# Queries of two latent heads projected and their rotary parts transposed together

## The chip, the cores and the metric

The kernel runs on one core of one Trainium2 chip. The metric is the device time of one execution in microseconds (us), as a median of several executions; lower is better. The engines are named as the profile names them: PE (TensorE, matmuls), PEld (its weight loads), DVE (VectorE), ACT (ScalarE), POOL (GpSimd) and SP (SyncE, which issues DMAs).

## The reference

One decoder layer over 1024 tokens of 1024 features: a SwiGLU block, a mixer with two groups of heads, and a second SwiGLU block. The change lies in the second group of the mixer, multi-head latent attention with four heads of 128 + 64 query columns:

```python
q = (_rms(cq, q_a_norm) @ w_q_b).reshape(B, S, H, MLA_QK_DIM)          # H = 4, 192 columns a head
kv = (_rms(ckv, kv_a_norm) @ w_kv_b).reshape(B, S, H, MLA_NOPE + MLA_V_DIM)
k = jnp.concatenate([k_nope, k_pe], axis=-1)
q, k = _rms(q, q_g), _rms(k, k_g)
q = jnp.concatenate([q[..., :MLA_NOPE], _rope(q[..., MLA_NOPE:], pos)], axis=-1)
k = jnp.concatenate([k[..., :MLA_NOPE], _rope(k[..., MLA_NOPE:], pos)], axis=-1)
```

followed by causal softmax attention of each head. `cq` has 256 features, so a query tile is a sum over two blocks of 128. Every product of exact operands is made of three matmuls on a high and a low part of each operand.

## The kernel before

The program is one long list that a scheduler puts in order at build time; each engine then runs its own list, and semaphores hold an instruction back until what it reads or overwrites is ready. The stages follow each other: first SwiGLU, projections, twelve attention heads, output projection, second SwiGLU.

The attention stage walks over `order`, a list of (head, item): eight dilated heads with eight pairs of tiles each, then four latent heads with eight query tiles each (the last head in reverse). An item has four steps: scores `s` (lines 838 and 890), exponential `e` (846, 903), transposes `t` (854, 914) and values `v` (864, 929); `t` runs three items behind `s`, and `v` four. Between the steps `behind` advances jobs. A job is a generator with a start, an end and a number of steps, and at each call it is moved on in proportion to the place reached in `order`. `merge` (lines 1258 to 1260) is such a job: it combines the near and far halves of the dilated heads. `prep_mla` is another: it prepares the latent heads, from `MSTART` on, with 75 steps spread up to one head before the end of the list.

For each head and each half of the tokens (four tiles, `th`) `prep_mla` does the following, with a `yield` after each piece. It projects the keys and values (two banks of PSUM, 256 columns a tile, `products`, lines 122 to 126) and takes the squares of the keys on ACT (1157). It runs what is left of the half before (`late`: transposes of the keys). It projects the queries, two tiles of 192 columns to a bank and two banks a half; DVE multiplies a bank with the gain (1172) and ACT squares it (1175). Behind the first query bank DVE scales the keys (1179), ACT copies the values (1183) and POOL scales the keys' rotary part (1185). DVE rotates the queries' rotary part in six instructions (1101 to 1106). PE transposes the queries' first 128 columns (`turn_nope`, line 1052) and then the rotary 64 (`turn_rope`, 1052), each with four transposes; ACT copies the high part of the rotary result to the upper 64 partitions of `qs` (1117), and DVE writes the low part to the other 64 (1118). POOL makes the queries' inverse norms (1192 to 1194) and rotates the keys (1101 to 1106). `late` transposes the keys in the same way and has two DMAs on POOL's queue swap halves of `k1` into `k2` (1205, 1206).

All tiles of 4 KB a partition come from a pool of 47 buffers (`slot`), and PSUM has 8 banks (`ps`).

Of the kernel before, what the change touches and what calls it, by code (L numbers as in the profile page):

```python
# [10 lines left out]
F32 = mybir.dt.float32  # L11
# [41 lines left out]
MSTART = 6.5  # L53
# [8 lines left out]
def tile_layer(ctx: ExitStack, tc: tile.TileContext, x, g1n, mixn, g2n, wg1, wu1, wd1, wg2, wu2, wd2,  # L62
# [985 lines left out]
    def four_turns(src, rows_, hi, lo):  # L1048

        tp = ps()  # L1050
        for i in range(4):
            nc.tensor.transpose(tp[:rows_, i * P:(i + 1) * P], src(i), ident)  # L1052
        if rows_ == P:
            split(hi, lo, tp)
        return tp
# [40 lines left out]
    def rotary(eng, y, th, o):  # L1096

        cos, sin = mla["cs"][:, 4 * th:4 * th + 4, 0:32], mla["cs"][:, 4 * th:4 * th + 4, 32:64]
        a, b = y[:, :, 0:32], y[:, :, 32:64]
        w = tmp([P, 2, 4, 32])  # L1100
        eng.tensor_tensor(o[:, :, 0:32], a, cos, op=ALU.mult)
        eng.tensor_tensor(w[:, 0], b, sin, op=ALU.mult)
        eng.tensor_tensor(o[:, :, 32:64], b, cos, op=ALU.mult)
        eng.tensor_tensor(w[:, 1], a, sin, op=ALU.mult)
        eng.tensor_tensor(o[:, :, 0:32], o[:, :, 0:32], w[:, 0], op=ALU.subtract)
        eng.tensor_tensor(o[:, :, 32:64], o[:, :, 32:64], w[:, 1], op=ALU.add)
# [3 lines left out]
    def turn_nope(y, th, nope):  # L1110
        sl = slice(th * 512, (th + 1) * 512)
        four_turns(lambda i: y[:, i, :NOPE], P, nope[0][:, sl], nope[1][:, sl])

    def turn_rope(ro, th, rope):
        sl = slice(th * 512, (th + 1) * 512)
        tp = four_turns(lambda i: ro[:, i, :], ROPE, None, None)
        nc.scalar.activation(rope[:ROPE, sl], tp[:ROPE, :], AF.Copy)
        nc.vector.tensor_tensor(rope[ROPE:, sl], tp[:ROPE, :], rope[:ROPE, sl].bitcast(F32), op=ALU.subtract)

    def mla_head(h):  # L1120
        qn, kn = ((slot([P, 1024], F32R), slot([P, 1024], F32R)) for _ in range(2))
        qs, k1, k2 = (slot([P, 1024], F32R) for _ in range(3))
        vh = slot([P, NT, P])
        rq = [(small(4), small(4)) for _ in range(2)]
# [16 lines left out]
        return qn, kn, qs, k1, k2, vh, rq  # L1141

    def prep_mla():


        late = iter(())
        for h in range(MH):
            cT, wq, wkv = mla["c"], mla["wq"], mla["wkv"]
            qn, kn, qs, k1, k2, vh, rq = mla_head(h)
            for th in range(2):  # L1150
                yk, yq, ro, ss, pk = slot([P, 4, QK]), slot([P, 4, QK]), tmp([P, 4, ROPE]), small(4), []
# [12 lines left out]
                sq = small(4)  # L1164
                for b in range(2):
                    pq = ps()
                    for i in range(2):
                        t, o = 4 * th + 2 * b + i, pq[:, i * QK:(i + 1) * QK]
                        products(o, [(cut(cT[k], t * P, (t + 1) * P), cut(wq[k], h * QK, (h + 1) * QK))
                                     for k in range(2)])  # L1170
                    yv = yq[:, 2 * b:2 * b + 2, :]
                    nc.vector.tensor_tensor(yv, pq[:, :2 * QK].rearrange("p (i c) -> p i c", i=2),
                                            mla["gq"][:, None, :].to_broadcast([P, 2, QK]), op=ALU.mult)
                    for i in range(2):
                        nc.scalar.activation(pq[:, i * QK:(i + 1) * QK], pq[:, i * QK:(i + 1) * QK], AF.Square,
                                             accum_out=sq[:, 2 * b + i:2 * b + i + 1])
                    if b == 0:
                        for i in range(4):
                            nc.vector.scalar_tensor_tensor(
# [275 lines left out]
```

## Time and profile before

| | us |
|---|---|
| median of 3 runs | 1834.58 (1834.56 to 1834.69) |
| the profiled execution | 1836.06 |
| span of its instructions | 1834.3 |
| PE busy | 1807.4, 9040 instructions |
| DVE busy | 1240.9, 2375 instructions |
| ACT busy | 785.9, 1794 instructions |
| POOL busy | 305.8, 528 instructions |

The profiled execution took 1.5 us more than the median, of which 1.8 us lie around the span. Busy time counts an engine's instructions from start to modelled end, so matmuls that overlap in the pipeline count once, and a PE that is 99% busy can still wait for up to some 0.15 us at a time without a gap in the count. How often matmuls start says more than how long one lasts.

### The profile page before, as it was taken

What the parts mean: (1) busy time and instruction counts of PE and PEld (TensorE: products, weight loads), DVE (VectorE), ACT (ScalarE), POOL (GpSimd) and SP (SyncE); (2) the same over time, 40 slices, a digit from 0 to 9 for tenths busy, and PEclk for the clock granted to TensorE, in tenths of its full rate; (3) what the DMA queues carried; (4) which work ended last, traced back from release to release, by engine and by line L of the source; (5) the groups of instructions that cost most, each with busy time, mean ns of one, the idle gap of its engine ahead of it and who ended that gap; (6) DMA issues with size and microseconds to landing.
All of it is one profiled execution on the core that took longest, in us unless ns stands there. A gap on an engine that the chain in (4) does not pass through costs nothing.

```text
span 1834.3 us, 25184 instructions
## 1 busy us (share of the span) xinstructions
PE 1807.4 (99%) x9040; PEld 1532.6 (84%) x9040; DVE 1240.9 (68%) x2375; ACT 785.9 (43%) x1794; POOL 305.8 (17%) x528
## 2 busy tenths in 40 slices
PE   8999999999999999999999999999999999999999
PEld 6888888888888888889998988888888888888887
DVE  6878776677967364337878783458777666687771
ACT  7532233333454343236876672364232333343540
POOL 3111110000000213332455530211111001000000
PEclk9999999999999999999999999999999999999999
DMA  7435452228943241023311332344345223387412
GB/s 287 163 113 185 145 187 90 98 77 292 342 127 92 99 131 35 29 69 116 87 33 36 84 113 95 125 167 137 132 165 190 86 93 120 134 300 272 127 51 92
DMA packets 95077, 243.82 MB, mean 133 GB/s; under 512 B 12934, under 2 KB 18776, under 8 KB 94952
## 3 DMA queue, kind: packets, MB, share of 16 engines
q1 hardware_dynamic: 72744, 167.12, 27.4%
q0 software_dynamic: 22208, 75.09, 12.0%
q8 instruction: 71, 1.16, 0.3%
q14 instruction: 54, 0.44, 0.1%
HBM read 172.34 MB, written 65.63 MB: 130 GB/s over the span
## 4 chain that ended last, share of the span: by engine, by line
PE 90%; DVE 3%; DMA 2%; ACT 2%; issue 1%; POOL 1%; SPq 0%; POOLq 0%; DVEq 0%; ACTq 0%
PE ps L122 20%; PE ps L124 20%; PE ps L126 20%; PE ps L524 7%; PE ps L523 7%; PE ps L522 7%; PE ps L864 2%; PE ps L929 1%; PE ps L890 1%; PE ps L838 1%; PE ps L854 1%; PE ps L1052 1%; DMA slot<-in_wu_dram 1%; PE ps L178 1%; ACT slot L101 1%
## 5 line engine op out<-in xcount | busy, mean ns | idle before, releaser
L122 PE MATMUL ps<-slot,slot 128*128 128x512 f32 (+3 forms) x1712 | 657.6, 385 | 3.1 <-DVE slot L218 1.6
L124 PE MATMUL ps<-slot,slot 128*128 128x512 f32 (+3 forms) x1712 | 654.0, 382 | 0.0
L126 PE MATMUL ps<-slot,slot 128*128 128x512 f32 (+3 forms) x1712 | 654.0, 382 | 0.0
L122 PEld LDWEIGHTS ps<-slot,slot 128*128 128x128 f32 x1712 | 322.0, 188 | 65.9 <-DVE slot L218 2.1
L126 PEld LDWEIGHTS ps<-slot,slot 128*128 128x128 f32 x1712 | 322.0, 188 | 61.8
L124 PEld LDWEIGHTS ps<-slot,slot 128*128 128x128 f32 x1712 | 322.2, 188 | 60.5
L102 DVE TENSOR_TENSOR slot<-slot,slot 128x512 fp32r<-128x512 f32 (+1 forms) x428 | 293.7, 703 | 40.6 <-ACT slot L101 38.8
L101 ACT ACTIVATE slot<-slot 128x512 fp32r<-128x512 f32 (+1 forms) x428 | 259.6, 638 | 98.9 <-PE ps L524 49.0
L101 ACT ACTIVATE slot<-tmp 128x512 fp32r<-128x512 f32 x258 | 160.8, 625 | 317.0 <-DVE tmp L332 137.3
L523 PE MATMUL ps<-slot,slot 128*128 128x512 f32 x616 | 239.8, 390 | 0.0
L524 PE MATMUL ps<-slot,slot 128*128 128x512 f32 x616 | 239.6, 389 | 0.0
L522 PE MATMUL ps<-slot,slot 128*128 128x512 f32 x616 | 237.2, 389 | 0.0
L102 DVE TENSOR_TENSOR slot<-tmp,slot 128x512 fp32r<-128x512 f32 x258 | 176.4, 686 | 21.7 <-ACT slot L101 21.6
L523 PEld LDWEIGHTS ps<-slot,slot 128*128 128x128 f32 x616 | 115.7, 188 | 24.1
L524 PEld LDWEIGHTS ps<-slot,slot 128*128 128x128 f32 x616 | 115.7, 188 | 23.9
L522 PEld LDWEIGHTS ps<-slot,slot 128*128 128x128 f32 x616 | 115.7, 188 | 23.8
L609 ACT ACTIVATE tmp<-tmp 128x512 f32<-128x512 f32 x76 | 48.1, 632 | 152.7 <-DVE tmp L601 72.8
L530 DVE SCALAR_TENSOR_TENSOR slot<-ps,slot 128x512 f32<-128x512 f32 x56 | 37.4, 687 | 81.1 <-PE ps L524 80.9
L846 ACT ACTIVATE slot<-slot,tmp 128x256 f32<-128x256 f32 (+1 forms) x128 | 59.7, 468 | 27.2 <-DVE tmp L839 26.4
L136 POOL TENSOR_TENSOR small<-small,neghalf 128x1 f32<-128x1 f32 (+2 forms) x68 | 66.8, 984 | 5.0
L592 DVE TENSOR_TENSOR tmp<-tmp,ps 128x512 f32<-128x512 f32 x44 | 30.2, 686 | 51.2 <-ACT tmp L588 50.7
L864 PE MATMUL ps<-slot,slot 128*128 128x64 f32 x432 | 56.3, 269 | 2.2 <-DVE slot L856 1.6
(180 smaller groups left out, 1962.8 us busy)
## 6 DMA issues: line engine op xcount, KB each, us to landing
tmp<-act SPq DMA_DIRECT2D x154, 256.0 KB
slot<-in_wg_dram SPq DMA_DIRECT2D x56, 512.0 KB
slot<-in_wu_dram SPq DMA_DIRECT2D x56, 512.0 KB
act<-slot POOLq DMA_DIRECT2D x54, 512.0 KB, 4.6
slot<-in_wd_dram SPq DMA_DIRECT2D x40, 512.0 KB
act<-slot POOLq DMA_DIRECT2D x34, 256.0 KB, 3.3
slot<-in_x_dram SPq DMA_DIRECT2D x16, 512.0 KB
x_mid<-slot POOLq DMA_DIRECT2D x16, 512.0 KB, 3.5
```

The source lines that it names most:

```text
L101: nc.scalar.activation(hi, src, AF.Copy)
L102: return nc.vector.tensor_tensor(lo, src, hi.bitcast(F32), op=ALU.subtract)
L122: pin(nc.tensor.matmul(pt, ah, bh, start=first and i == 0, stop=False, skip_group_check=not first))
L124: pin(nc.tensor.matmul(pt, ah, bl, start=False, stop=False, skip_group_check=not first))
L126: pin(nc.tensor.matmul(pt, al, bh, start=False, stop=i == total - 1, skip_group_check=not first))
L136: nc.gpsimd.tensor_tensor(r, r, neghalf[:, :w], op=ALU.pow)
L522: nc.tensor.matmul(banks[i], ah, w[:, 0, :], start=first and k == 0, stop=False, skip_group_check=not first)
L523: nc.tensor.matmul(banks[i], ah, w[:, 1, :], start=False, stop=False, skip_group_check=not first)
L524: nc.tensor.matmul(banks[i], al, w[:, 0, :], start=False, stop=k == KD - 1, skip_group_check=not first)
L609: nc.scalar.activation(q, q, AF.Silu)
L846: nc.scalar.activation(self.p[:, e, :w], self.p[:, e, :w], AF.Exp, bias=self.m[e], scale=-1.0, accum_out=self.den[e])
L864: nc.tensor.matmul(po[:, e * HD:(e + 1) * HD], self.pt[:, n * P:(n + 1) * P], self.head["values"](self.far, self.j, e, j - nb + 1), start= ...
```

## The change

Heads are prepared in pairs. For an even head, the tiles of both heads' queries are allocated together (`queries`), and for each half of the tokens the queries of this head and the next are projected in one product of 384 columns a tile (four banks, one a tile, two blocks of 128 features, three matmuls each). The gain, the squares and the rotation work on both heads at once in pieces of the same number of elements as before. The rotary parts of both heads (2 x 64 columns) of a tile are transposed by one transpose; the result has the first head in the lower 64 partitions and the second in the upper, and ACT and DVE then write high and low parts for each head. For an odd head only keys and values are left. `MSTART` goes from 6.5 to 6.

```diff
-MSTART = 6.5
+MSTART = 6
...
-    def turn_rope(ro, th, rope):
+    def turn_rope(src, th, ropes):
+
         sl = slice(th * 512, (th + 1) * 512)
-        tp = four_turns(lambda i: ro[:, i, :], ROPE, None, None)
-        nc.scalar.activation(rope[:ROPE, sl], tp[:ROPE, :], AF.Copy)
-        nc.vector.tensor_tensor(rope[ROPE:, sl], tp[:ROPE, :], rope[:ROPE, sl].bitcast(F32), op=ALU.subtract)
+        tp = four_turns(src, ROPE * len(ropes), None, None)
+        for i, rope in enumerate(ropes):
+            own, other = (slice(j * ROPE, (j + 1) * ROPE) for j in (i, 1 - i))
+            nc.scalar.activation(rope[own, sl], tp[own, :], AF.Copy)
+            nc.vector.tensor_tensor(rope[other, sl], tp[own, :], rope[own, sl].bitcast(F32), op=ALU.subtract)
...
+    def queries():
+        return (slot([P, 1024], F32R), slot([P, 1024], F32R)), slot([P, 1024], F32R), [(small(4), small(4)) for _ in range(2)]
...
-            qn, kn, qs, k1, k2, vh, rq = mla_head(h)
+            if h % 2 == 0:
+                two = [queries() for _ in range(2)]
+            kn, k1, k2, vh = mla_head(h, *two[h % 2])
...
-                for b in range(2):
-                    pq = ps()
-                    for i in range(2):
-                        t, o = 4 * th + 2 * b + i, pq[:, i * QK:(i + 1) * QK]
-                        products(o, [(cut(cT[k], t * P, (t + 1) * P), cut(wq[k], h * QK, (h + 1) * QK))
-                                     for k in range(2)])
...
+                rok = tmp([P, 4, ROPE])
+                if h % 2:
+                    keys()
                     yield
...
+                    rotary(nc.gpsimd, yk[:, :, None, NOPE:], 4 * th, rok[:, :, None])
+                else:
+                    yq, ro, sq = [slot([P, 2, 2, QK]) for _ in range(2)], tmp([P, 4, 2, ROPE]), [small(4) for _ in range(2)]
+                    for i in range(4):
+                        t, pq = 4 * th + i, ps()
+                        products(pq[:, :2 * QK], [(cut(cT[k], t * P, (t + 1) * P), cut(wq[k], h * QK, (h + 2) * QK))
+                                                  for k in range(2)])
+                        nc.vector.tensor_tensor(yq[i // 2][:, i % 2], pq[:, :2 * QK].rearrange("p (j c) -> p j c", j=2),
+                                                mla["gq"][:, None, :].to_broadcast([P, 2, QK]), op=ALU.mult)
+                        for j in range(2):
+                            o = pq[:, j * QK:(j + 1) * QK]
+                            nc.scalar.activation(o, o, AF.Square, accum_out=sq[j][:, i:i + 1])
+                        if i == 0:
+                            keys()
+                        yield
+                    for j in range(2):
+                        rotary(nc.vector, yq[j][:, :, :, NOPE:], 4 * th + 2 * j, ro[:, 2 * j:2 * j + 2])
+                        turn_nope(lambda i: yq[i // 2][:, i % 2, j, :NOPE], th, two[j][0])
+                        yield
+                    for j in range(2):
+                        r, nr = two[j][2][th]
+                        nc.gpsimd.tensor_scalar(r, sq[j], 1.0 / QK, EPS, op0=ALU.mult, op1=ALU.add)
+                        nc.gpsimd.tensor_tensor(r, r, neghalf[:, :4], op=ALU.pow)
+                        nc.gpsimd.tensor_scalar(nr, r, -1.0, None, op0=ALU.mult)
+                    rotary(nc.gpsimd, yk[:, :, None, NOPE:], 4 * th, rok[:, :, None])
+                    turn_rope(lambda i: ro[:, i].rearrange("p j c -> p (j c)"), th, [q[1] for q in two])
+                    yield
```

`keys()` holds the three edits on the keys (lines 1175 to 1182 of the kernel after) that stood behind the first query bank.

Three places of the scheduled lists show how the work moves. The first is PE's list in a group of query products. `slot_6950` and `slot_6951` are the high and low part of the normed latent features 0 to 127, `slot_7017` and `slot_7018` those of features 128 to 255, and `slot_7156` to `slot_7159` the query weights. Before, the six rows make one tile of one head:

```order
L122 MATMUL ps_8842<-slot_6950,slot_7156 128x192
L124 MATMUL ps_8842<-slot_6951,slot_7156 128x192
L126 MATMUL ps_8842<-slot_6950,slot_7157 128x192
L122 MATMUL ps_8842<-slot_7017,slot_7158 128x192
L124 MATMUL ps_8842<-slot_7018,slot_7158 128x192
L126 MATMUL ps_8842<-slot_7017,slot_7159 128x192
```

Now six rows make one tile of two heads:

```order
L122 MATMUL ps_9002<-slot_6950,slot_7156 128x384
L124 MATMUL ps_9002<-slot_6951,slot_7156 128x384
L126 MATMUL ps_9002<-slot_6950,slot_7157 128x384
L122 MATMUL ps_9002<-slot_7017,slot_7158 128x384
L124 MATMUL ps_9002<-slot_7018,slot_7158 128x384
L126 MATMUL ps_9002<-slot_7017,slot_7159 128x384
```

The number of weight loads halves, and each matmul has twice the columns.

The second place is DVE's list around the eight multiplications of `merge` (`slot_5409` to `slot_5412` are the outputs of the dilated heads, `tmp_5413` their weights; the line is 1258 before and 1274 after). Before:

```order
L1258 TENSOR_TENSOR slot_5409<-slot_5409,tmp_5413 128x512 x2
L1258 TENSOR_TENSOR slot_5410<-slot_5410,tmp_5413 128x512 x2
L1258 TENSOR_TENSOR slot_5411<-slot_5411,tmp_5413 128x512 x2
L1258 TENSOR_TENSOR slot_5412<-slot_5412,tmp_5413 128x512 x2
L102 TENSOR_TENSOR slot_8475<-ps_8790,slot_8474 128x512
L916 COPY slot_8603<-ps_8818 128x384
L891 ISA slot_8800,small_8801<-ps_8802,slot_6834 128x512
```

After:

```order
L891 ISA slot_8797,small_8798<-ps_8806,slot_6834 128x256
L891 ISA small_8798 128x1
L1274 TENSOR_TENSOR slot_5409<-slot_5409,tmp_5413 128x512 x2
L1274 TENSOR_TENSOR slot_5410<-slot_5410,tmp_5413 128x512 x2
L1274 TENSOR_TENSOR slot_5411<-slot_5411,tmp_5413 128x512 x2
L1274 TENSOR_TENSOR slot_5412<-slot_5412,tmp_5413 128x512 x2
L896 SCALAR_TENSOR_TENSOR small_8813<-small_8798,small_7932 128x1
L924 RECIPROCAL small_8820<-small_8666 128x1
L1175 SCALAR_TENSOR_TENSOR slot_8729<-ps_8731,small_8784,slot_6829 128x128 x2
L1175 SCALAR_TENSOR_TENSOR slot_8729<-ps_8764,small_8784,slot_6829 128x128 x2
L1122 TENSOR_TENSOR slot_8568<-ps_8822,slot_8568 64x512
```

The burst stays in one piece; behind it now stand the scaling of the keys (`slot_8729`) and the low part of a rotary result (`ps_8822`), where before a low part of the keys (`ps_8790`) and two steps of items stood.

The third place is PE's list from the score matmul that the burst follows (`ps_8806`) to the transposes of the keys `slot_8729`, in the kernel after. Left out are further matmuls of the product whose first row is shown:

```order
L890 MATMUL ps_8806<-slot_7944,slot_7929 128x256
L122 MATMUL ps_8764<-slot_7088,slot_7160 128x256
...
L1052 MATMUL ps_8822<-ident,tmp_8714 64x128 x4
L929 MATMUL ps_8834<-slot_7945,slot_8607 128x128 x2
L122 MATMUL ps_8874<-slot_7088,slot_7160 128x256
...
L890 MATMUL ps_8885<-slot_7941,slot_7927 128x512
...
L890 MATMUL ps_8892<-slot_7941,slot_7927 128x384
...
L914 MATMUL ps_8901<-ident,slot_8682 128x128 x4
L122 MATMUL ps_8909<-slot_7088,slot_7160 128x256
...
L1052 MATMUL ps_8922<-ident,slot_8729 128x128 x4
```

Before, the same stretch of PE's list ended in the queries of one head (`ps_8842`, shown above, then `ps_8865`), ahead of scores of the first latent head (`ps_8883`, `ps_8890`) and of the queries' own transposes (`slot_8755`, `tmp_8756`):

```order
L122 MATMUL ps_8865<-slot_6950,slot_7156 128x192
...
L890 MATMUL ps_8883<-slot_8021,slot_8019 128x512
...
L890 MATMUL ps_8890<-slot_8021,slot_8019 128x384
...
L914 MATMUL ps_8899<-ident,slot_8666 128x128 x4
L1052 MATMUL ps_8914<-ident,slot_8755 128x128 x2
L929 MATMUL ps_8926<-slot_8026,slot_8603 128x128 x3
L1052 MATMUL ps_8942<-ident,tmp_8756 64x128 x4
```

So behind the burst PE now comes to the keys' transposes where it came to the second bank of one head's queries, and the queries follow later, for two heads at once.

The lists of both kernels are alike up to the first key product of `prep_mla` among the dilated heads, and again late in the last latent head; SP's list has the same order throughout.

More of the change, by code (lines that the diff above doesn't have):

```diff
@@ L1052, in four_turns @@
             nc.tensor.transpose(tp[:rows_, i * P:(i + 1) * P], src(i), ident)
-        if rows_ == P:
+        if hi is not None:
             split(hi, lo, tp)
@@ L1094, in prep_c, with rotary @@
                 yield
[L1096 to L1106, printed above, removed]
+    def rotary(eng, y, t, o):
+        n, m = y.shape[1:3]
+        cos, sin = (mla["cs"][:, t:t + n, None, c:c + 32].to_broadcast([P, n, m, 32]) for c in (0, 32))
+        a, b = y[:, :, :, 0:32], y[:, :, :, 32:64]
+        w = [x.rearrange("p (t h c) -> p t h c", t=n, h=m) for x in (lambda x: (x[:, 0], x[:, 1]))(tmp([P, 2, P]))]
+        eng.tensor_tensor(o[:, :, :, 0:32], a, cos, op=ALU.mult)
+        eng.tensor_tensor(w[0], b, sin, op=ALU.mult)
+        eng.tensor_tensor(o[:, :, :, 32:64], b, cos, op=ALU.mult)
+        eng.tensor_tensor(w[1], a, sin, op=ALU.mult)
+        eng.tensor_tensor(o[:, :, :, 0:32], o[:, :, :, 0:32], w[0], op=ALU.subtract)
+        eng.tensor_tensor(o[:, :, :, 32:64], o[:, :, :, 32:64], w[1], op=ALU.add)
@@ L1123, in mla_head @@
+    def queries():
+        return (slot([P, 1024], F32R), slot([P, 1024], F32R)), slot([P, 1024], F32R), [(small(4), small(4)) for _ in range(2)]
+    def mla_head(h, qn, qs, rq):
+        kn = (slot([P, 1024], F32R), slot([P, 1024], F32R))
+        k1, k2 = (slot([P, 1024], F32R) for _ in range(2))
         vh = slot([P, NT, P])
-        rq = [(small(4), small(4)) for _ in range(2)]
         def scores(qt, half, w):
@@ L1198, in prep_mla, with keys @@
-                yield
+                def keys(yk=yk, pk=pk, rk=rk, th=th, vh=vh):
+                    for i in range(4):
+                        nc.vector.scalar_tensor_tensor(
+                            yk[:, i, :NOPE], pk[i // 2][:, i % 2 * 256:i % 2 * 256 + NOPE], rk[:, i:i + 1],
+                            mla["gk"][:, :NOPE], op0=ALU.mult, op1=ALU.mult)
+                    for b2 in range(2):
+                        nc.scalar.activation(vh[:, 4 * th + 2 * b2:4 * th + 2 * b2 + 2, :],
+                                             pk[b2].rearrange("p (j c) -> p j c", j=2)[:, :, NOPE:], AF.Copy)
+                    nc.gpsimd.tensor_tensor(yk[:, :, NOPE:], mla["kp"][:, 4 * th:4 * th + 4, :],
+                                            rk[:, :, None].to_broadcast([P, 4, ROPE]), op=ALU.mult)
```

45 lines of the change are left out of this document (8 added, 37 removed).

## The prediction

> **What bounds the kernel now.** I read the page's busy shares and its chain of waits first, then the stretches of the attention stage, then who waited for whom in the part that the change touches.
>
> ```profile
> PE 1807.4 (99%) x9040; PEld 1532.6 (84%) x9040; DVE 1240.9 (68%) x2375; ACT 785.9 (43%) x1794; POOL 305.8 (17%) x528
> PE 90%; DVE 3%; DMA 2%; ACT 2%; issue 1%; POOL 1%; SPq 0%; POOLq 0%; DVEq 0%; ACTq 0%
> ```
>
> PE is the bound of the whole: 99% busy and 90% of the chain. The averages hide the stage in question. By stretches (length, then busy time of PE, PEld, DVE, ACT, POOL, then the granted clock):
>
> ```profile
> 910.00:960.00 50.00, 48.53 (x424) 47.76 (x424) 40.28 (x140) 40.06 (x164) 23.52 (x44) 1.00 0.16 38
> 960.00:1000.00 40.00, 36.66 (x270) 34.18 (x268) 35.50 (x110) 25.98 (x91) 22.79 (x43) 0.96 0.20 45
> 1000.00:1060.00 60.00, 59.72 (x461) 56.44 (x460) 48.32 (x150) 39.71 (x131) 33.23 (x58) 1.00 0.30 87
> 1100.00:1160.00 60.00, 60.00 (x293) 50.35 (x292) 22.79 (x43) 15.53 (x38) 5.69 (x15) 1.00 0.25 90
> ```
>
> The reader should see that PE never rests in the second SwiGLU (60.00 of 60), and that from 910 to 1060 us, where the latent heads are prepared, DVE is close behind it: 40.28 of 50, then 35.50 of 40. PE time saved there is time saved as long as DVE keeps up. What PE waited for in 834 to 1060 us (total, times, longest), the rows over 1.3 us:
>
> ```profile
> PE ps L1052 <- DVE tmp L1106: 2.5, 4, 1.3
> PE ps L864 <- DVE slot L856: 1.6, 3, 0.7
> PE ps L122 <- DVE slot L102: 1.4, 1, 1.4
> ```
>
> All end with DVE. Two of these waits stand together, at the one place where DVE has a block of work that cannot be broken up:
>
> ```profile
> 973.91 4.90 DVE L1258 TENSOR_TENSOR slot<-slot,tmp 128x512 f32<-128x512 f32 x8
> 978.72 0.68 DVE L102 TENSOR_TENSOR slot<-ps,slot 128x512 fp32r<-128x512 f32 x1
> ...
> 980.39 0.42 DVE L891 CUSTOM_DVE_ANT_0 slot<-ps,slot 128x256 f32<-128x256 f32 x1
> 980.85 0.68 DVE L1118 TENSOR_TENSOR slot<-ps,slot 64x512 fp32r<-64x512 f32 x1
> 981.57 1.12 DVE L1179 SCALAR_TENSOR_TENSOR slot<-ps,small,slot 128x128 f32<-128x128 f32 x4
> 982.61 1.53 DVE L896 SCALAR_TENSOR_TENSOR small<-small,small 128x1 f32<-128x1 f32 x1
> ```
>
> ```profile
> 979.46 0.36 PE L122 MATMUL ps<-slot,slot 128*128 128x192 f32 x1 [1.43 <-DVE slot L102]
> 987.58 0.60 PE L1052 MATMUL ps<-ident,tmp 128*64 128x128 f32 x4 [1.35 <-DVE tmp L1106]
> 979.50:983.50 4.00, 4.00 (x17) 3.61 (x18) 3.94 (x11) 0.77 (x2) 3.61 (x7) 0.57 0.31 66
> ```
>
> The eight multiplications of `merge` hold DVE for 978.72 - 973.91 = 4.81 us. The queries' products behind them wait 1.43 us, and the rotary transposes later 1.35 us. Right after the first wait the granted clock is 0.57 over 4 us, which loses 0.43 x 4 = 1.7 us. I call this place the burst.
>
> **The change part by part.** First the products. The timeline of PE gives starts, and so the pace:
>
> ```profile
> 994.26 0.27 PE L126 MATMUL ps<-slot,slot 128*128 128x192 f32 x1
> ...
> 996.61 0.27 PE L126 MATMUL ps<-slot,slot 128*128 128x192 f32 x1
> ```
>
> ```profile
> 1057.48 1.04 PE L890 MATMUL ps<-slot,slot 128*128 128x384 f32 x5
> 1058.35 0.38 PE L914 MATMUL ps<-ident,slot 128*128 128x128 f32 x2
> ```
>
> ```profile
> 1006.89 1.32 PE L890 MATMUL ps<-slot,slot 128*128 128x512 f32 x5
> 1008.05 0.27 PE L914 MATMUL ps<-ident,slot 128*128 128x128 f32 x1
> ```
>
> From the first quoted start to the last lie 21 matmuls of 192 columns: 2.35 / 21 = 0.112 us each. Five of 384 columns take 0.87 us, 0.174 each, and five of 512 take 1.16, 0.232 each. So a matmul of 192 columns costs more than its columns (192/512 of 0.232 is 0.087), and one of 384 costs 0.174 where two cost 0.224. Before there are 4 heads x 8 tiles x 6 = 192 of them, now 96 of 384: 192 x 0.112 - 96 x 0.174 = 21.5 - 16.7 = **4.8 us** less on PE.
>
> The Trainium skill has a rule that speaks against this ("TensorE: Matmul & The Clock Gate", section "Back-to-back issue gap"): an isolated matmul of N columns takes N/2.4 ns plus 2.5, which makes 82.5 ns for 192 columns and 162.5 for 384, an estimate of 2.5 ns saved a pair and 0.24 us in all. The same page's section on LDWEIGHTS gives the columns of the weights over 1.2, 107 ns for 128, which with the measured 0.112 says that the loads set the pace here; the measurement decides.
>
> Second, the transposes and what DVE and ACT do with them:
>
> ```profile
> L1052 PE MATMUL ps<-ident,tmp 128*64 128x128 f32 x64 | 9.7, 274 | 2.5 <-DVE tmp L1106 2.5
> 993.62 0.60 PE L1052 MATMUL ps<-ident,tmp 128*64 128x128 f32 x4
> ```
>
> Half of the 64 transposes are of queries. A group of four spans 0.60 us, of which the last takes 0.27, so they start (0.60 - 0.27)/3 = 0.11 apart; 16 go, and those that stay have 128 stationary columns in place of 64. The transposes of 128 columns are quoted nowhere as slower: their rows (L914 above, two in 0.38) give the same 0.38 - 0.27 = 0.11. So 16 x 0.11 = **1.8 us** less.
>
> DVE, ACT and POOL keep their counts: 16 products with the gain, 48 rotary steps on DVE, 16 pairs of copies and subtractions for rotary parts, 32 squares. Their access changes:
>
> ```profile
> L1172 DVE TENSOR_TENSOR slot<-ps,slot 128x384 f32<-128x384 f32 x16 | 8.7, 551 | 2.2 <-PE ps L126 2.1
> L856 DVE COPY slot<-ps 128x384 f32<-128x384 f32 x40 | 22.1, 554 | 3.2 <-PE ps L854 2.9
> L1101 DVE TENSOR_TENSOR tmp<-slot,slot 128x128 f32<-128x128 f32 x8 | 2.9, 368 | 0.2
> L1105 DVE TENSOR_TENSOR tmp<-tmp,tmp 128x128 f32<-128x128 f32 x8 | 2.4, 295 | 0.0
> L1118 DVE TENSOR_TENSOR slot<-ps,slot 64x512 fp32r<-64x512 f32 x16 | 10.9, 684 | 2.8 <-ACT slot L1117 2.4
> L983 DVE TENSOR_TENSOR slot<-slot,slot 64x512 fp32r<-64x512 f32 x8 | 6.2, 769 | 0.3
> ```
>
> A gain repeated over two tiles costs nothing against a plain copy (551 against 554 ns), so I expect nothing from the repeated cosines; the rotary rows bound it by 368 - 295 = 73 ns, 48 x 0.07 = 3.5 us of DVE at most. The second head's low part goes from the upper 64 partitions to the lower. L983 does this for half of its heads, at 769 against 684 ns, so the bound is 8 x 0.09 = 0.7 us. Below, both are bounded by nothing, since the element counts stay. I take 0 for both; ahead of PE they are covered by PE's own work except at the burst.
>
> Third, the order. `MSTART` and the pairing move DVE work forward among the dilated heads, and at the burst other work now waits. Behind it PE needs the scaled keys and the bank that a rotary subtraction frees. DVE then has, from the score reduction ahead of the burst: 0.42 + 4.81 + small ones 0.2 + the keys 1.04 (981.57 to 982.61) + the rotary subtraction 0.72 (980.85 to 981.57) = 7.2 us. PE meanwhile has three products of the keys (9 matmuls, 1.1 at the 0.12 of 256 columns in proportion), four rotary transposes 0.44, two value blocks 0.45, ten score matmuls 5 x 0.232 + 5 x 0.174 = 2.0, and four transposes 0.44: 4.4 us. Its wait is 7.2 - 4.4 = 2.8 us, with some 0.3 from matmul to DVE 3.1. This takes the place of 1.43 + 1.35 = 2.8, so the burst costs 0.3 more, and its clock loss I leave as it is. Queued behind the waiting transposes are the values of an item and the rotary transposes of the keys; nothing but PE itself waits for those at once.
>
> Among the dilated heads the query work now comes ahead of PE's need for it, but each dilated item also needs DVE twice. A wait there looks like this:
>
> ```profile
> 936.43 0.60 PE L1052 MATMUL ps<-ident,tmp 128*64 128x128 f32 x4 [0.59 <-DVE tmp L1106]
> ```
>
> I add one more of these, 0.6. It could be none or, by the count of the waits quoted above (4 + 3 + 1), as many as eight, 4.7 us; I take one because the four rotary waits become four again, with two heads' worth of rows in each.
>
> The sum is 4.8 + 1.8 - 0.3 - 0.6 = 5.7 us. The profiled execution's 1836.06 becomes 1830.4; it stands 1.5 above the median of 1834.58, which becomes **1828.9**.
>
> **The clock** at the burst: the trace shows the clock at 0.57 after a wait of 1.43 us, and no such stretch after the 1.35. The Trainium skill (same page, "Part 1: The HAM clock gate", the table of two states) has half clock only after an idle window of about 3.4 us. By that rule the new wait of 3.1 us would cost no clock and the 1.7 us would be won; the trace shows loss after a shorter wait, and I keep it.
>
> **The rivals.**
>
> *DVE becomes the bound of more places.* The 1.6 us a group that PE saves (6.6 / 4 groups) only brings it to DVE sooner. For it: 35.50 of 40 us in the latent stretch. Against it: 48.32 of 60 after that. Price: one more wait of the burst's kind, 1.4, and one more stretch at low clock, 1.7: 5.7 - 3.1 = 2.6 us, 1832.0.
>
> *The burst meets PE less hard.* PE's list there has its long products behind the wait, not ahead. If the wait halves (1.4 won) and the clock stays up (1.7), then 6.6 + 3.1 = 9.7: 1824.9.
>
> *The change does not do what it says on PE*: the pace goes by columns alone. By the 512-column rows 192 columns would be 0.087 and a pair 0.174, the same as one of 384, so only 1.8 us are left, less 0.9: 1833.7. [...] The measured 0.112 speaks against it.
>
> *Buffers run short, and it gets slower.* Four more tiles of the pool of 47 are held: three of the second head's queries and a second query tile. If the score tile of an item must wait for the values of the item four back, PE stands for one passage through reduction, exponential, transposes and copy:
>
> ```profile
> L891 DVE CUSTOM_DVE_ANT_0 slot<-ps,slot 128x512 f32<-128x512 f32 x16 | 10.9, 686 | 4.5 <-PE ps L890 4.5
> L903 ACT ACTIVATE slot<-slot,small,small 128x512 f32<-128x512 f32 x15 | 12.1, 810 | 4.7 <-DVE small L924 1.9 <-POOL small L1192 1.1 <-DVE small L896 1.1
> L916 DVE COPY slot<-ps 128x512 f32<-128x512 f32 x10 | 6.8, 683 | 0.0
> ```
>
> That is 0.69 + 0.81 + 0.6 (four transposes) + 0.68 = 2.8, with the clock 4.5 us each time. It decides from three times on: 13.5 - 5.7 = 7.8 us slower, 1842.4; twice it is 3.3 slower, which is within 0.2%. Against it: PE's list has scores, transposes and values at the same distances as before.
>
> **How the numbers follow.** 0.2% is 3.7 us, about what a measurement of this kernel can tell from no change. Chances: the forecast 0.61, DVE's rival 0.22, the gentler burst 0.08, pace by columns 0.02, buffers 0.07. The forecast's own range is 1826.5 to 1831.2 and has nearly all of its chance under 1830.9. Faster: 0.58 of the forecast and 0.08, 0.66. Same: 0.03 + 0.22 + 0.02 = 0.27. Slower: 0.07. The range reaches from near the gentler burst, 1825.5, to just over the two small gains, 1834.0. It leaves out the buffers and the far end of the gentler burst. The eight small waits at 0.59 (1833.0), and 3.5 us on DVE if all of it reached PE (1832.4), lie in it.
>
> **What would show it.** In the profile after: 96 query matmuls of 384 columns starting 0.174 apart with four transposes fewer a group, which confirm the 6.6; PE's wait behind the eight multiplications, one of about 3 us, at the keys' transposes; the granted clock there; rotary steps at 0.30 to 0.37 us. The time from the last score tile of the latent heads to the end should not move. The prediction is wrong if PE's waits from 910 to 1060 us grow by more than 2 us, or if low clock shows in a second place.

## The result, and the profile after

| | before | after |
|---|---|---|
| median | 1834.63 us (1834.56 to 1835.15, 4 runs) | 1845.51 us (1845.06 to 1846.81, 4 runs) |
| ratio, 95% interval | | 1.0058 (1.0046 to 1.0070) |
| the profiled execution | 1836.06 us, span 1834.3 | 1845.06 us, span 1843.3 |

The change costs 10.9 us. The forecast was 5.7 us faster, and the time lies above its range. The two profiled executions differ by 9.0 us, and it is this difference that the traces can account for. The page of the kernel after begins with busy times and shares of the chain:

```profile
PE 1804.7 (98%) x8928; PEld 1528.4 (83%) x8928; DVE 1241.7 (67%) x2375; ACT 785.0 (43%) x1794; POOL 308.5 (17%) x528
PE 89%; DVE 4%; DMA 2%; ACT 2%; issue 1%; POOL 1%; SPq 0%; DVEq 0%; POOLq 0%; ACTq 0%
```

PE has the 112 instructions less that were counted (96 products, 16 transposes), DVE has as much to do as before (1241.7 against 1240.9 us), and the chain lists one more hundredth of DVE. In the three stretches of the latent stage (length, then busy time of PE, PEld, DVE, ACT, POOL, then the granted clock):

```profile
910.00:960.00 50.00, 48.36 (x390) 46.77 (x388) 43.17 (x154) 39.72 (x166) 25.88 (x49) 1.00 0.16 36
960.00:1000.00 40.00, 33.03 (x215) 30.88 (x214) 31.91 (x91) 22.61 (x83) 21.53 (x38) 0.87 0.18 37
1000.00:1060.00 60.00, 52.12 (x377) 48.50 (x376) 41.89 (x136) 36.38 (x123) 30.02 (x51) 0.97 0.21 65
```

From 960 to 1000 us PE stands for 7.0 us where it stood for 3.3, and from 1000 to 1060 for 7.9 where it stood for 0.3; DVE's share fell at the same time (31.91 of 40 against 35.50, 41.89 of 60 against 48.32). Both engines wait more. The clock is low in both stretches, where it was low in one. The last value matmul of the latent heads, from the view of its line in both kernels (before, then after):

```profile
L929 PE MATMUL ps<-slot,slot x288: 271/275/378, 971.5 to 1120.5; 128*128 128x128 f32 x144
```

```profile
L929 PE MATMUL ps<-slot,slot x288: 272/275/421, 972.1 to 1129.4; 128*128 128x128 f32 x144
```

It comes 8.9 us later, of 9.0 in the span: the whole loss is made before it. What PE waited for from 905 to 1065 us (total, times, longest):

```profile
PE ps L1052 <- DVE slot L1122: 6.9, 1, 6.9
PE ps L1052 <- DVE tmp L1107: 3.4, 1, 3.4
PE ps L914 <- ACT slot L1179: 1.3, 1, 1.3
PE ps L929 <- DVE slot L916: 1.2, 1, 1.2
PE ps L122 <- ACT slot L1165: 0.9, 1, 0.9
```

With five rows of 0.4 to 0.7 that view adds up to 16.3 us; before it was 4.8. The two largest waits are the two places to look at. First the burst, from the timeline (start, length, then in brackets the wait that ended there); L1274 are the eight multiplications of `merge`:

```profile
975.06 0.40 PE L890 MATMUL ps<-slot,slot 128*128 128x256 f32 x2
...
978.24 0.42 DVE L891 CUSTOM_DVE_ANT_0 slot<-ps,slot 128x256 f32<-128x256 f32 x1
...
978.58 6.46 DVE L1274 TENSOR_TENSOR slot<-slot,tmp 128x512 f32<-128x512 f32 x8
...
980.03 0.29 PE L126 MATMUL ps<-slot,slot 128*128 128x256 f32 x1
980.23 0.81 POOL L1102 TENSOR_TENSOR tmp<-slot,slot 128x128 f32<-128x128 f32 x1
...
984.45 0.89 POOL L1107 TENSOR_TENSOR tmp<-tmp,tmp 128x128 f32<-128x128 f32 x1
...
985.36 1.10 DVE L1175 SCALAR_TENSOR_TENSOR slot<-ps,small,slot 128x128 f32<-128x128 f32 x4
...
986.49 0.68 DVE L1122 TENSOR_TENSOR slot<-ps,slot 64x512 fp32r<-64x512 f32 x1
...
987.23 1.11 PE L1052 MATMUL ps<-ident,slot 128*128 128x128 f32 x4 [6.91 <-DVE slot L1122]
```

The order is the one forecast: PE comes to the keys' transposes while DVE is in the block. Two numbers are not. The score that the block follows is finished on PE at 975.46, but DVE takes it at 978.24, 2.8 us later. And the block takes 6.46 us, not 4.81, while GpSimd rotates keys beside it. A part of the lag could be seen before, where the score ahead of the block ended on PE at 971.06 and DVE took it 1.8 us later:

```profile
969.06 2.00 PE L890 MATMUL ps<-slot,slot 128*128 128x512 f32 x10
...
972.83 0.29 DVE L891 CUSTOM_DVE_ANT_0 slot<-ps,slot 128x128 f32<-128x128 f32 x1
```

In the kernel after, DVE has also waited 0.8 us for a load of `merge_weights`, the job that prepares `merge` (L1250, at 973.33); before, it had no such wait there. Then the clock, in stretches cut to fit:

```profile
987.23:993.22 5.99, 5.99 (x26) 5.84 (x27) 3.32 (x9) 2.70 (x10) 1.60 (x3) 0.50 0.22 48
1033.40:1038.90 5.50, 4.91 (x19) 4.13 (x20) 4.25 (x12) 0.80 (x2) 3.66 (x7) 0.69 0.26 97
```

PE works at half clock for 6.0 us behind the first wait (3.0 us lost) and at 0.69 for 5.5 us behind the second (1.7 lost); before, there was one such stretch, with 1.7. The second place, at the rotary transposes of the queries of latent heads 2 and 3:

```profile
1028.40 0.28 DVE L1102 TENSOR_TENSOR tmp<-slot,slot 128x128 f32<-128x128 f32 x1
...
1030.00 0.29 DVE L1105 TENSOR_TENSOR tmp<-slot,slot 128x128 f32<-128x128 f32 x1
1030.00 0.60 PE L1052 MATMUL ps<-ident,slot 128*128 128x128 f32 x4
...
1031.67 0.69 DVE L1275 TENSOR_TENSOR slot<-slot,tmp 128x512 f32<-128x512 f32 x1 [1.38 <-DMA slot<-o_far]
1032.28 0.28 DVE L1106 TENSOR_TENSOR tmp<-tmp,tmp 128x128 f32<-128x128 f32 x1
1032.44 1.26 POOL L1276 TENSOR_TENSOR slot<-slot,slot 128x512 f32<-128x512 f32 x1 [7.45 <-DVE slot L1275]
1032.48 0.68 DVE L916 COPY slot<-ps 128x512 f32<-128x512 f32 x1
1033.08 0.77 DVE L1107 TENSOR_TENSOR tmp<-tmp,tmp 128x128 f32<-128x128 f32 x1
...
1033.99 0.50 PE L1052 MATMUL ps<-ident,tmp 128*128 128x128 f32 x2 [3.39 <-DVE tmp L1107]
```

Between the fourth and the fifth of the six rotary steps that PE waits for stands L1275, `merge`'s multiplication of a far half. It waits 1.38 us for its load, and the rotation waits behind it, and PE behind the rotation. The sixth step, L1107, takes 0.77 us in place of 0.28 beside L1276, `merge`'s addition on GpSimd.

### The profile page after: what moved, and what is told of

Its sections match the earlier page's. It is cut to its first block, busy times and chain, and to the rows that moved or that the text cites. A ratio compares the mean times of both kernels' runs of the same rounds, so it can differ in the third digit from the quotient of the medians.

```text
span 1843.3 us, 24964 instructions
## 1 busy us (share of the span) xinstructions
PE 1804.7 (98%) x8928; PEld 1528.4 (83%) x8928; DVE 1241.7 (67%) x2375; ACT 785.0 (43%) x1794; POOL 308.5 (17%) x528
## 4 chain that ended last, share of the span: by engine, by line
PE 89%; DVE 4%; DMA 2%; ACT 2%; issue 1%; POOL 1%; SPq 0%; DVEq 0%; POOLq 0%; ACTq 0%
PE ps L122 20%; PE ps L126 20%; PE ps L124 20%; PE ps L523 7%; PE ps L524 7%; PE ps L522 7%; PE ps L864 2%; PE ps L929 1%; PE ps L890 1%; PE ps L838 1%; PE ps L854 1%; DMA slot<-in_wu_dram 1%; PE ps L178 1%; ACT slot L101 1%; PE ps L914 0%
## 5 line engine op out<-in xcount | busy, mean ns | idle before, releaser
L122 PEld LDWEIGHTS ps<-slot,slot 128*128 128x128 f32 x1680 | 316.1, 188 | 65.0 <-DVE slot L218 2.1
L126 PEld LDWEIGHTS ps<-slot,slot 128*128 128x128 f32 x1680 | 316.0, 188 | 61.7
L124 PEld LDWEIGHTS ps<-slot,slot 128*128 128x128 f32 x1680 | 316.3, 188 | 61.0
L523 PEld LDWEIGHTS ps<-slot,slot 128*128 128x128 f32 x616 | 115.6, 188 | 24.1
L522 PEld LDWEIGHTS ps<-slot,slot 128*128 128x128 f32 x616 | 115.6, 188 | 24.1
L524 PEld LDWEIGHTS ps<-slot,slot 128*128 128x128 f32 x616 | 115.6, 188 | 23.7
L838 PE MATMUL ps<-slot,slot 128*128 128x256 f32 x256 | 56.7, 317 | 1.7 <-DVE tmp L839 1.7
```

The costliest lines, as they stand in the source:

```text
L122: pin(nc.tensor.matmul(pt, ah, bh, start=first and i == 0, stop=False, skip_group_check=not first))
L124: pin(nc.tensor.matmul(pt, ah, bl, start=False, stop=False, skip_group_check=not first))
L126: pin(nc.tensor.matmul(pt, al, bh, start=False, stop=i == total - 1, skip_group_check=not first))
L522: nc.tensor.matmul(banks[i], ah, w[:, 0, :], start=first and k == 0, stop=False, skip_group_check=not first)
L523: nc.tensor.matmul(banks[i], ah, w[:, 1, :], start=False, stop=False, skip_group_check=not first)
L524: nc.tensor.matmul(banks[i], al, w[:, 0, :], start=False, stop=k == KD - 1, skip_group_check=not first)
```

## The experiments

Theory 1: what stands on DVE ahead of the keys' scaling and between the rotary steps, `merge`'s multiplications above all, makes the loss. Rival 2: the pairing does it, because the first rotary transposes of a pair need four gains and twelve rotary steps where those of one head needed two and six. Rival 3: the earlier start does it alone. Times are medians; the kernel before measured 1834.8 to 1835.3 beside them, up to 0.7 above the 1834.63 of the result, so a difference from the 1845.51 of the kernel after is uncertain by as much.

| | start | us | ratio to before, 95% | longest waits of PE, 905 to 1065 us |
|---|---|---|---|---|
| e1 near behind far | 6 | 1840.37 | 1.0017 to 1.0041 | 4.3, 2.6 |
| e2 products single | 6 | 1850.36 | 1.0066 to 1.0096 | 6.9, 5.3 |
| e3 turns single | 6 | 1843.62 | 1.0029 to 1.0063 | 7.0, 3.5 |
| e4 before, earlier start | 6 | 1845.45 | 1.0040 to 1.0070 | 5.1, 2.7 |
| e5 e1, far held too | 6 | 1836.65 | 1.0000 to 1.0019 | 2.7, 1.1 |
| e6 e5, later turns | 6 | 1847.84 | 1.0057 to 1.0087 | 4.8, 3.2 |
| e7 before, held | 6.5 | 1836.87 | 1.0002 to 1.0020 | 2.1, 1.0 |
| e8 after, other start | 6.25 | 1841.83 | 1.0025 to 1.0054 | 3.7, 3.2 |
| e9 no rotation beside the block | 6 | 1845.72 (one run) | | 5.6, 3.6 |
| e10 e5, other start | 6.25 | 1843.29 | 1.0031 to 1.0061 | 2.0, 1.7 |
| e11 e5, turns single | 6 | 1834.62 | 0.9990 to 1.0009 | 1.0, 0.8 |
| e12 e11, merge ends earlier | 6 | 1843.73 | 1.0035 to 1.0063 | 7.5, 2.2 |

**e1: the block taken apart.**

```diff
-            nc.vector.tensor_tensor(near, near, w[0], op=ALU.mult)
-            nc.vector.tensor_tensor(f, f, w[1], op=ALU.mult)
+            scaled = nc.vector.tensor_tensor(f, f, w[1], op=ALU.mult)
+            with tc.issue_after(scaled.ins):
+                nc.vector.tensor_tensor(near, near, w[0], op=ALU.mult)
```

> The kernel after, with each tile's near multiplication of merge held on DVE's list behind that tile's far multiplication, which needs the far half from memory; so the eight multiplications no longer stand in one piece ahead of the keys' scaling. Theory 1 (the block on DVE, with the keys' scaling and a rotary subtraction queued behind it, makes the loss): the wait of 6.9 us goes down to 1.5 or less and the clock stays at 1.00 there, which gives back 5.4 us and about 2.9 us of clock: 1837 us, and less if the later waits go with it. Rival 2 (the pairing itself: four query tiles of two heads must be ready before the first rotary transposes, wherever the block stands): the wait moves to the next transposes and the time stays within 2 us of 1845.5.

Measured 1840.37 us, 5.1 less than after, of 8.5 expected. The waits of the kernel e1:

```profile
PE ps L1052 <- DVE tmp L1107: 4.3, 1, 4.3
PE ps L929 <- DVE slot L102: 2.6, 1, 2.6
```

The wait of 6.9 us is gone, and no low clock shows there; so the block made that wait. But the wait at the second place grew from 3.4 to 4.3, with two multiplications now between the rotary steps. Neither expectation holds whole: some of the time went where rival 2 said, at a place where theory 1 can act too.

**e2 and e3: each half of the change undone, at the start of 6.**

```diff
-                        products(pq[:, :2 * QK], [(cut(cT[k], t * P, (t + 1) * P), cut(wq[k], h * QK, (h + 2) * QK))
-                                                  for k in range(2)])
+                        for j in range(2):
+                            products(pq[:, j * QK:(j + 1) * QK], [(cut(cT[k], t * P, (t + 1) * P), cut(wq[k], (h + j) * QK, (h + j + 1) * QK))
+                                                                  for k in range(2)])
```

> The kernel after, with the 96 query matmuls of 384 columns made as 192 of 192 columns again, all else as it is. If the forecast's 4.8 us of PE are really in the kernel after and lie where PE is the bound: 1850.3 us. If PE waits for DVE where the products stand (theory 1 at the burst and behind it), part of the added PE time fills waits: 1847 to 1849. If the pace of the matmuls of 384 columns gave nothing (pace by columns alone): 1845.5.

Measured 1850.36, 4.85 more than after, as if the products' 4.8 us were in the kernel after. The pace of the products in the kernel after:

```profile
1020.04 0.34 PE L126 MATMUL ps<-slot,slot 128*128 128x384 f32 x1
...
1021.63 0.33 PE L126 MATMUL ps<-slot,slot 128*128 128x384 f32 x1
```

These are nine steps in 1.59 us, 0.177 each, where the forecast took 0.174. So 192 x 0.112 - 96 x 0.177 = 4.5 us are gone from PE's list. The agreement of the totals is luck: in e2 the wait at the second place is also longer (5.3 us against 3.4), the rows of waits add up to 17.8 us against 16.3, and there is one more stretch of low clock.

```diff
-                    turn_rope(lambda i: ro[:, i].rearrange("p j c -> p (j c)"), th, [q[1] for q in two])
+                    for j in range(2):
+                        turn_rope(lambda i: ro[:, i, j], th, [two[j][1]])
```

> The kernel after, with the queries' rotary parts transposed head by head again (16 more transposes, the same copies and subtractions, both heads' results in the lower 64 partitions), the products still in 384 columns. If the forecast's 1.8 us are there: 1847.3 us. Rival 2 (the transposes of both heads wait for the rotation of both): a shorter chain for the first head gives back up to the 3.4 us wait: 1842 to 1845.

Measured 1843.62, 1.9 less than after, though PE has 16 transposes more. But the wait at the second place did not move (3.5 us against 3.4), so rival 2's mechanism is not seen at work there. What went are later waits: those of 1.3 for L1179 and 0.9 for L1165 in the rows of after above have no counterpart in e3, which has one of 1.1 for a rotary subtraction there. The transposes of both heads in one were worth less than nothing here, by an arrangement of waits that I did not take further apart.

**e4: the earlier start alone.** In the kernel before:

```diff
-MSTART = 6.5
+MSTART = 6
```

> The kernel before with MSTART 6 in place of 6.5, the start of the latent heads' preparation alone. Theory 1: its list has three other rows inside the block and no scaled keys directly behind it, so no long wait: 1834 to 1838 us. Rival 3 (the earlier start alone makes the loss, the pairing has no part in it): 1843 to 1848.

Measured 1845.45: as slow as the change, against theory 1 and for rival 3. Its waits:

```profile
PE ps L1052 <- DVE tmp L1106: 6.6, 3, 5.1
PE ps L1052 <- DVE small L896: 2.7, 1, 2.7
```

They stand elsewhere, though: the first at 928 us, among the dilated heads, where PE comes to the rotary transposes of one head while DVE has this ahead of it:

```profile
929.04 0.45 DVE L1101 TENSOR_TENSOR tmp<-slot,slot 128x128 f32<-128x128 f32 x1
929.42 0.54 DVE L1102 TENSOR_TENSOR tmp<-slot,slot 128x128 f32<-128x128 f32 x1
...
930.90 0.69 DVE L983 TENSOR_TENSOR slot<-slot,slot 64x512 fp32r<-64x512 f32 x1
931.62 0.42 DVE L839 CUSTOM_DVE_ANT_0 slot<-ps,slot 128x256 f32<-128x256 f32 x1
...
933.12 0.28 DVE L1106 TENSOR_TENSOR tmp<-tmp,tmp 128x128 f32<-128x128 f32 x1
```

The low part of a dilated head's queries (L983) and the scores of a dilated item (two of L839) have come between the rotary steps. So at this start both kernels are 10 us slower than the kernel before, by different waits. The start alone can make such a loss; that it made this one is not shown, since the waits are not the same.

**e5: the far multiplications held as well.** `mark[0]` is the last low part of a rotary result (`turn_rope`) emitted so far:

```diff
-            scaled = nc.vector.tensor_tensor(f, f, w[1], op=ALU.mult)
+            with tc.issue_after(mark[0]):
+                scaled = nc.vector.tensor_tensor(f, f, w[1], op=ALU.mult)
...
-            nc.vector.tensor_tensor(rope[other, sl], tp[own, :], rope[own, sl].bitcast(F32), op=ALU.subtract)
+            mark[0] = nc.vector.tensor_tensor(rope[other, sl], tp[own, :], rope[own, sl].bitcast(F32), op=ALU.subtract).ins
```

> The kernel of e1 (the near multiplications behind the far ones), with each far multiplication also held on DVE's list behind the last low part of a rotary result emitted before it, so that it no longer stands between the rotary steps of the queries of latent heads 2 and 3, where it waits 1.4 to 1.7 us for its load. Theory 1b (the 4.4 us wait that stayed in e1 is this load ahead of the last rotary steps): the wait falls to about 1.5, and with 2 us of clock 1835 to 1837 us. Rival 2 (four gains and twelve rotary steps between the products of two heads and their first rotary transposes are too long a chain for the distance that PE's list gives them): the wait stays over 3 us and the time at 1839 to 1841.

Measured 1836.65, as theory 1 expected; 8.9 of the 10.9 us are back. At the second place PE now waits

```profile
PE ps L1052 <- DVE tmp L1107: 1.1, 1, 1.1
```

with four gains and ten of the twelve rotary steps still ahead of the first transposes. Rival 2's chain is worth about 1 us there. DVE waits for no load of a far half between 905 and 1065 us in e5. As far as the traces name its instructions, PE's list is that of the kernel after but for 33 of its 8928 places. The longest wait that is left, 2.7 us at 1035.88, stands behind four of the held multiplications: the hold moved them to a place where they cost less.

**e6: rotary transposes later.** They move from the end of the queries' steps to the start of `last`:

```diff
-                    turn_rope(lambda i: ro[:, i].rearrange("p j c -> p (j c)"), th, [q[1] for q in two])
+                    turns = lambda ro=ro, th=th, two=two: turn_rope(
+                        lambda i: ro[:, i].rearrange("p j c -> p (j c)"), th, [q[1] for q in two])
                     yield
...
+                    if turns:
+                        turns()
+                        yield
```

> The kernel of e5, with the queries' rotary transposes moved behind the next half's first key products (to the start of what is run late), so that PE comes to them later. Rival 2 (the chain is too long for the distance): PE's waits at rotary transposes go below 1 us in all, and the time falls to 1829 to 1832, below the kernel before. Theory 1b alone: no more than 1 us from e5.

Measured 1847.84, a plain miss: 11.2 us more than e5. With `turn_rope` later, `mark[0]` is older when a multiplication is emitted, and it no longer holds it back. The longest wait (4.8 us) starts at 1031 us, and on DVE at that time stand

```profile
1029.49 0.69 DVE L1279 TENSOR_TENSOR slot<-slot,tmp 128x512 f32<-128x512 f32 x1 [1.93 <-DMA slot<-o_far]
...
1032.16 0.69 DVE L1279 TENSOR_TENSOR slot<-slot,tmp 128x512 f32<-128x512 f32 x1 [1.38 <-DMA slot<-o_far]
```

With a near one (L1281) behind each, these are four multiplications with two waits for loads, in front of the score reductions (L891) that PE waits for. So this run tells nothing of rival 2; it shows theory 1's mechanism at another place.

**e7 and e8: the hold in the kernel before, and another start in the kernel after.** e7 has the edits of e1 and e5 in the kernel before; e8 has only `MSTART = 6.25` in the kernel after.

> The kernel before with the same two edits on merge as e5 (near behind far, both behind a low part of a rotary result), nothing else. The prediction priced the block there at waits of 1.43 and 1.35 us and 1.7 us of clock: without it 1830 to 1832 us. If the same wait for DVE comes up elsewhere: 1834 to 1837.

> The kernel after with MSTART 6.25, its work and its pairing unchanged. If what the change loses is a matter of where the preparation's steps fall among the items' steps (which the start shifts), the waits move to other places and the time moves by several us either way: outside 1843 to 1848. If the pairing itself sets the loss: within 1843 to 1848.

e7: 1836.87, no gain but 1.8 us more (its profiled execution, 1835.94, was one of its faster ones and shows no loss to explain). The waits at the burst became others, the longest 2.1 us for a rotary step:

```profile
PE ps L1052 <- DVE tmp L1106: 3.8, 4, 2.1
```

Taking the multiplications away from one place puts them at another, and in the kernel before they stood no worse. e8: 1841.83, 3.7 us less than at a start of 6, outside the band that would have meant that the pairing sets the loss. Where the steps fall is worth several us.

**e9: the block without GpSimd's rotation.** For latent head 1 and the second half of the tokens:

```diff
+                    if (h, th) == (1, 1):
+                        nc.gpsimd.tensor_copy(rok, yk[:, :, NOPE:])
+                    else:
+                        rotary(nc.gpsimd, yk[:, :, None, NOPE:], 4 * th, rok[:, :, None])
```

> The kernel after without the rotation of the keys of latent head 1 for the second half of the tokens (six instructions of GpSimd, which ran beside the block of eight multiplications; one copy of GpSimd stands in their place, so these keys come out unrotated). If GpSimd's work beside the block is what stretched it from 4.81 us before to 6.46 us: 4.8 to 5.3 us, each multiplication 0.60 us after the last, and PE's wait behind it 5.0 to 5.7 us. If something else stretched it: 6.2 us or more. The whole time hangs on how the following rows fall: 1841 to 1846 us.

The block (L1277 here), what GpSimd does beside it, and the wait behind it:

```profile
979.22 5.30 DVE L1277 TENSOR_TENSOR slot<-slot,tmp 128x512 f32<-128x512 f32 x8
...
980.85 0.71 POOL L1189 COPY tmp<-slot 128x256 f32<-128x256 f32 x1
...
986.52 1.11 PE L1052 MATMUL ps<-ident,slot 128*128 128x128 f32 x4 [5.55 <-DVE slot L1122]
```

5.30 us in place of 6.46, and a wait of 5.55 in place of 6.91: GpSimd's work beside the block stretched it, since the lists of PE and DVE are the same in both. The whole time did not fall with it (1845.72 against 1845.51, one run): PE came to the second place earlier and waited 3.6 us there in place of 3.4, and more at other places.

**e10, e11 and e12: e5 with other edits.** e10 has `MSTART = 6.25`; e11 the transposes of e3; e12 is e11 with

```diff
-    jobs.append(Job(merge(range(NT)), 12, DH + 1, DH + 3))
+    jobs.append(Job(merge(range(NT)), 12, DH + 1, DH + 2.5))
```

> The kernel of e5 (merge's multiplications held behind the rotary results) with MSTART 6.25. The e8 waits at the block (3.35 us, one of 3.87 later) hang on the same multiplications: without them 1833 to 1836 us from e8's 1841.8. If the start alone decides where waits come up: no better than e5, 1836 to 1840.

> The kernel of e5 with the rotary transposes head by head again, as in e3. If the shorter chain of the first head is worth what it was in e3 (1.9 us): 1834 to 1835.5. If e3's gain lay in waits that e5 has taken away already, the 16 transposes cost their 1.8 us: 1838 to 1839.

> The kernel of e11 with merge's end a half head earlier (DH + 2.5 in place of DH + 3), so that its last multiplications stand farther ahead of the norm of the dilated heads, for whose transposes PE waits 4.0 us in e11. If those waits hang on merge's late end: 1.4 us less, 1833 us, just under the kernel before. If multiplications that stand closer together cost PE as much at other places: 1834 to 1838.

e10: 1843.29, no gain on e8, which has no hold (1841.83; their runs overlap). The hold is no remedy in itself: at this start one far multiplication waits 2.2 us for its load again. e11: 1834.62, the same as the kernel before, and the best that I found with the paired products; the 1.9 us of e3 came again (2.0). e12: 1843.73, where 1833 was hoped for. Its longest wait, and the far multiplications between the rotary steps that make it (a near one follows each):

```profile
PE ps L1052 <- DVE tmp L1107: 7.5, 1, 7.5
```

```profile
1022.57 0.28 DVE L1105 TENSOR_TENSOR tmp<-slot,slot 128x128 f32<-128x128 f32 x1
1024.49 0.69 DVE L1276 TENSOR_TENSOR slot<-slot,tmp 128x512 f32<-128x512 f32 x1 [1.63 <-DMA slot<-o_far]
...
1027.16 0.69 DVE L1276 TENSOR_TENSOR slot<-slot,tmp 128x512 f32<-128x512 f32 x1 [1.18 <-DMA slot<-o_far]
...
1028.37 0.28 DVE L1102 TENSOR_TENSOR tmp<-slot,slot 128x128 f32<-128x128 f32 x1
```

This was not meant, but it makes a series, of kernels that differ in other edits too. With none, one, two and four of `merge`'s multiplications, with their waits for loads, ahead of that group's first finished rotation (e5, after, e1, e12) PE waits there 1.1, 3.4, 4.3 and 7.5 us.

## Why the prediction was wrong

**PE's savings were right.** 112 instructions went; 384 columns take 0.177 us a matmul against 0.174 forecast, which makes 4.5 us on PE's list for the 4.8 forecast; with the products undone the time is 4.85 us more, but part of that is waits. The 1.8 us of the transposes are counted (16 fewer on PE's list) and in no time: undoing them made the kernel faster.

**The burst was mis-sized in two terms**, "7.2 - 4.4 = 2.8 us, with some 0.3 from matmul to DVE 3.1". PE's side held: from the score at 975.46 to the end of its list ahead of the transposes (980.03 + 0.29) are 4.9 us, against 4.4. DVE's side is 987.17 - 978.24 = 8.9 in place of 7.2, of which some 1.6 are the block, 6.46 long where I took the 4.81 of before, with no look at what GpSimd's list has beside it. And the sum starts DVE at the moment when PE has written the score; DVE was 2.8 us behind. 2.8 + 8.9 - 4.9 gives 6.8, the measured 6.9. A forecast of who waits for whom needs the lag between the engines at the start of the stretch, and a trace of the kernel before gives it only as far as the order is the same: there it was 1.8 us. Against the 2.8 us of the two waits before, the burst costs 4.1 us more, not 0.3.

**The term "I add one more of these, 0.6" failed as a step**, not only in size. It priced the moves behind the burst by small waits of the kernel before. What the order brought there is a wait of another kind: a multiplication of `merge` between two rotary steps, which waits for a load. The trace of before shows such waits of DVE, and I did not price them, because no work of PE hung on them there:

```profile
1027.54 0.69 DVE L1259 TENSOR_TENSOR slot<-slot,tmp 128x512 f32<-128x512 f32 x1 [1.76 <-DMA slot<-o_far]
```

This wait of before, 1.76 us, is longer than the one of after, 1.38, which together with the multiplication, a copy, the slowed rotary step and the clock behind it cost 3.4 + 1.7 us.

**The clock term** "I leave as it is" failed: 3.0 us at the burst and 1.7 at the second place, for 1.7 before. By the clock that is missing in them, the stretches at 0.50 last 3.4 us (before), 10.2 and 3.4 (after), and e7, with a wait of 2.1 us, has none. By the page of the Trainium skill that the prediction weighed, "TensorE: Matmul & The Clock Gate", "Part 1: The HAM clock gate", half clock comes after at least one idle window of about 3.4 us, and the window runs freely. The trace agrees for the wait of 6.9 us, which is long enough to hold a whole window, and in the length of the pieces. It does not agree for the wait of 1.43 us before, which is shorter than a window and had a piece at 0.50 behind it. So the prediction did well not to count on the 1.7 us by that rule; its term failed because the wait was 6.9 us and not 3.1, and because there was a second place.

**The edit of the start had no term of its own.** The prediction names it with the pairing, as what moves DVE work forward, and has one small wait of 0.6 us for both. e4 shows what it can do: 10.2 us in the kernel before (1845.45 against 1835.3 beside it), with nothing else changed. e8 shows 3.7 us for a quarter of a head.

**The sum.** PE's rows of waits from 905 to 1065 us rise by 11.5 us (16.3 - 4.8), the clock costs 3.0 more (3.0 + 1.7 - 1.7), and 6.6 are taken as saved: 7.9 of the 8.9 us by which the last value matmul is late. The rest lies in gaps that the rows of that view leave out, and in waits later on. Of the rivals, "DVE becomes the bound of more places" has the mechanism and was priced at 3.1 us where 14.5 were due; "buffers run short" has a time near the result, but e11 holds the same tiles and equals the kernel before. Both signs that the prediction named against itself came: waits up by more than 2 us, and low clock at a second place.

**Two readings that the sum does not use.** The stretch from 1100 to 1160 us, read there as the second SwiGLU, holds the end of the latent heads (the last value matmul starts at 1120.5) and the output projection. And the block "that cannot be broken up" is one by its order alone: e1 takes it apart.

**What stays open.** e5 shows that 8.9 of the 10.9 us hang on where `merge`'s multiplications stand at a start of 6. Since e4, e8 and e12 move the time by 3.7 to 10 us through order alone, it is the traces of the two places, more than that total, which say why. That the rest is the chain of two heads is not shown: e3 and e11 gain 1.9 and 2.0 us without it, but by other waits. The change with the old start of 6.5 was not tried. e11 has the paired products and only equals the kernel before. Its rows of waits from 905 to 1065 us add up to 6.7 us against 4.8, and it has no low clock there, so they do not say where the saved time went. No version was found that beats the kernel before.

## What to carry to other kernels

Before an engine's saved time is counted, list for each of its waits in the changed order what stands on the other engine ahead of the releasing instruction, with that engine's lag at the start, whatever else runs beside it, and the loads that its queue may stop for. A job that nobody waits for (here `merge`) still sets the time when its instructions fall between two steps that somebody waits for; hold it behind them by an explicit order rather than by where it happens to be emitted, and read the order again after each edit, since e6, e10 and e12 lost that hold by edits elsewhere. When an edit that changes no work (a start, an end of a job) moves the time by more than the edit under study, compare versions at several such settings before either is believed.

## What the runs showed of the hardware

**DVE and GpSimd hold each other up.** In the block after, the first three multiplications start 0.60 us apart, with GpSimd idle or issuing a DMA. The others, beside GpSimd's rotation, start 0.86 apart, and GpSimd's steps 0.86 too, where they start 0.42 apart elsewhere; both read two operands from SBUF. In e9 the pace returns to 0.60 as soon as GpSimd is done. In e4 DVE's rotary steps beside GpSimd start 0.46 apart, where the group at 1028 us above has 0.20. The Trainium skill ("SBUF — State Buffer", "Who interferes with whom") says that a DVE instruction with two SBUF inputs contends with a GpSimd instruction that reads SBUF, because its second input comes through the shared read port, and it calls the shared ports an exclusive lock. The turns after agree with that, though 0.86 is less than 0.60 + 0.42. The block of before shows another pattern: there GpSimd's small addition took 2.04 us, where the median of its eight is 0.20, and ended with the block, while the multiplications kept their pace of 0.60.

```profile
976.82 2.04 POOL L1160 TENSOR_TENSOR small<-small,kpss 128x4 f32<-128x4 f32 x1 [4.89 <-ACT slot L1157]
```

**The low clock comes in pieces of one length.** Read in steps of half a microsecond, the stretches of low clock from 905 to 1100 us, in all these runs that have any, lack 1.7, 3.4 or 5.1 us of clock, which at 0.50 is 3.4, 6.8 or 10.2 us. So a wait that sets it off costs PE up to 1.7 us more for each piece in which PE has work, and waits of 1.4 and 2.1 us did (before) and did not (e7).
